# A two-layer hybrid decoder trunk: transposes and sums of gate logarithms moved from TensorE to VectorE, and the order of some projections and of w_out changed

## The chip, the cores and the metric

The kernel runs on one core of one Trainium2 chip. The metric is the device time of one execution in microseconds (us). Before the change it is 941.57 us, the median of three runs (941.54 to 941.61).

## The reference, cut to what matters

`x` has 256 rows of 2048. Each of two layers normalises the rows, multiplies them by `w_in` (2048 x 7700), sends the columns to four groups of four heads, gates each group's output, and multiplies the four outputs, side by side, by `w_out` (2048 x 2048):

```
h = rms_norm(x, norm_g);  p = split_columns(h @ w_in)
fox  = forgetting_attention(q, k, v, log_sigmoid(p["fox_f"] + fox_fb))       * silu(p["fox_g"])
diff = rms_norm((softmax(q1 k1^T) - lam * softmax(q2 k2^T)) v, diff_norm_g)  * silu(p["diff_g"])
moba = softmax(q k^T) v, causal (256 rows are one block of keys)             * silu(p["moba_g"])
gla  = rms_norm(gla_chunked(q, k, v, log_a), gla_norm_g)                     * silu(p["gla_g"])
       log_a = log_sigmoid(p["gla_a"] @ gla_wa2 + gla_ba) / 16
       inside a chunk: scores[t,s] = sum_d q[t,d] k[s,d] exp(cum[t,d] - cum[s,d]), cum = cumsum(log_a)
x = x + concat([fox, diff, moba, gla]) @ w_out
```

A last `rms_norm` with `final_norm_g` ends it. All of it is float32.

## The kernel before, in words

**Weights in steps.** The weights (160 MB) are read once, in 304 steps of at most 528 KB. A step holds two or four slabs of 128 rows of one block of columns (256 to 512 wide). Its raw slab is split in two rounded halves, `hi` (ScalarE, `hi_of`, line 399) and `lo` = raw - `hi` (VectorE, `lo_of`, line 402); the left side is split too (`hTp` for the normalised rows, `mTh` and `mTl` for the mixed groups). TensorE multiplies hi by hi, hi by lo and lo by hi into the PSUM tile `mm`. `raw`, `hi` and `lo` have four buffers each, and `prepare(i + 3)` is written ahead of `multiply` of step i, so the halves of a step are asked for three steps before TensorE reads them. A "rows" step of 512 columns is 12 matmuls of 512 columns; a "cols" step is 8 of 512 and 8 of 256.

**The order of the work.** Each engine works through its own list in the order in which the program was written, and that order is made in Python: the loop over `plan` (line 1369) writes prepare, settle (evacuates a finished block), multiply, and then `tick`, which lets each pending task (a generator) write a little more. `tick` lets tasks go on as long as the estimated work of VectorE and of ScalarE (`Costed`, line 176) is below a budget that grows with the estimated time of TensorE (`give_time`). A task that lacks an input stands at `until`. Steps of a layer come in the order of `_blocks`: gla, fox, diff, moba, then `w_out`; steps 0 to 151 are the first layer's, 152 to 303 the second's. A `w_out` block takes the groups in the order 3 (gla), 0 (fox), 1 (diff), 2 (moba).

**The side work.** What is not a weight matmul goes through two PSUM tiles called `side` (two banks each):

- `gla`, line 599: forms logarithms `gl` of the gates (rows by features), splits them in `gh` and `glo`, and multiplies both by the 0/1 matrix `a_r` (1152 columns, the constant "sets"), which gives for seven levels of halving the sum of logarithms between a row and its block's middle. ScalarE takes the exponential straight from PSUM into `ee`. VectorE multiplies it into q and k (`tq`, `ee`) and picks the scores with `masks`.
- Probabilities are transposed in `transposed_p` (line 753): on VectorE by `turned` (line 290, sixteen 32x32-block transposes for each group of tiles) when `by_rows` is true (fox alone), else as 12 transposes of 128x128 on TensorE (line 288) through `side`, which ScalarE and VectorE copy out.
- `finish_rows` (line 524) normalises and gates gla and diff; gla's result goes through `turned`, diff's through 8 TensorE transposes.
- `make_hT` (line 432) turns chunks of the residual rows `xs` for the next layer: chunks 0 to 2 on VectorE, chunk 3 on TensorE.

**The end.** The last block ("apart") finishes rows 0 to 127 first, then rows 128 to 255; `final_rows` (line 1135) adds the residual, sums squares, raises to -1/2 on GpSimd, scales 2048 columns on ScalarE and VectorE and sends them out in four pieces.

Of the kernel before, what the change touches and what calls it, by code (L numbers as in the profile page):

```python
# [13 lines left out]
F32 = mybir.dt.float32  # L14
F32R = mybir.dt.float32r
# [6 lines left out]
P = 128  # L22
SEQ = 256
D = 2048
# [38 lines left out]
def _constants():  # L63

    i = np.arange(P)
    tables, at = {"f": [], "b": []}, {}

    def put(name, a, kind="f"):
        parts = tables[kind]
        at[name] = (sum(x.shape[1] for x in parts), a.shape[1])  # L70
        parts.append(np.ascontiguousarray(a, TYPES[kind]))

    put("ident", np.eye(P))
    put("after", (i[:, None] > i[None, :]))
# [3 lines left out]
    sets, masks = [], []  # L78
    for h in GLA_LEVELS:
        blk, second = i // (2 * h), (i // h) % 2 == 1  # L80
        ref = blk * 2 * h + h - 1
        u, t = i[:, None], i[None, :]
        a = np.where(second[None, :], (u > ref[None, :]) & (u <= t), (u > t) & (u <= ref[None, :]))
        sets.append(a / GLA_TAU)
        masks.append(((blk[:, None] == blk[None, :]) & ~second[:, None])[:, second])
    sets += [(i[:, None] > i[None, :]) / GLA_TAU, (i[:, None] <= i[None, :]) / GLA_TAU]
    put("sets", np.concatenate(sets, 1), "b")
# [16 lines left out]
def _blocks():  # L104
# [6 lines left out]
    for l in range(DEPTH):  # L111
        for kind, c0, n in (
# [29 lines left out]
def _steps():  # L142

    steps = []
    for i, b in enumerate(_blocks()):
        per = b["per"]
        for j in range(0, KT, per):
            key = (j // 4, i) if i < 3 else (9, i)
            steps.append((key, len(steps), {"block": i, "kts": b["kts"][j:j + per], "first": j == 0, "last": j + per == KT,
                                           "odd": j // per % 2 == 1}))  # L150
    steps = [s for _, _, s in sorted(steps, key=lambda z: z[:2])]
    at = 0
    for s in steps:
        s["at"] = at
        at += P * len(s["kts"]) * _BLOCKS[s["block"]]["n"]
    return steps
# [61 lines left out]
def hybrid_trunk(  # L218
# [100 lines left out]
    ones_r = cp.tile([P, P], F32R, name="ones_r")  # L319
    a_r = cp.tile([P, (NL + 2) * P], F32R, name="a_r")  # L320
    neg_b = cp.tile([P, P], BF16, name="neg_b")
# [23 lines left out]
    def constants():  # L345
# [5 lines left out]
        s = []  # L351
        for name in ("sets", "upto", "masks"):
# [12 lines left out]
        yield  # L365
        v_.tensor_copy(a_r, s[0])
        v_.tensor_copy(upto_r, s[1])
        v_.tensor_copy(masks.rearrange("p l t -> p (l t)"), s[2])
        v_.tensor_scalar(ones_r, ident, 0.0, 1.0, op0=OP.mult, op1=OP.add)
# [154 lines left out]
    def finish_rows(l, gi, o, ops, scale, sg):  # L524
# [20 lines left out]
        yield  # L545
        if scale is None:
            t = yield from s4.take([P, H, SEQ])
            yield from turned(t.rearrange("p h (m t) -> p m h t", m=2), mixed.rearrange("p m (h d) -> p m h d", h=H))
            s4.put(mixed)
            yield from split_group(l, gi, t, lambda: s4.put(t))  # L550
            return
# [47 lines left out]
    def gla(l, an):  # L599
# [8 lines left out]
        al = yield from take_side()  # L608
        for m in range(2):
            matmul(al[:, m * 256:(m + 1) * 256], at17[:, m * P:(m + 1) * P], wa[:, l], True, True)  # L610
        yield
        e = yield from s2.take([P, 512])
        gl = yield from s2.take([P, 2, 256])
        yield from log_sigmoid(gl.rearrange("p m e -> p (m e)"), al[:, :512], e)
# [5 lines left out]
        yield  # L620
        glo = yield from s2.take([P, 2, 256], F32R)
        lo_of(glo, gl, gh)
        s2.put(gl)
# [20 lines left out]
        for pair in range(2):  # L644
            ee = yield from s8.take([P, 2, NL + 1, P])
            for m in range(2):
                pe = yield from take_side()
                for b in range(2):
                    for part in (gh, glo):
                        lhs = part[:, m, pair * P:(pair + 1) * P]  # L650
                        if b == 0:
                            matmul(pe[:, :512], lhs, a_r[:, 0:512], part is gh, part is glo)
                        elif m == 0:
                            matmul(pe[:, 512:], lhs, a_r[:, 512:1024], part is gh, part is glo)
                        else:
                            matmul(pe[:, 512:896], lhs, a_r[:, 512:896], part is gh, False)
                            matmul(pe[:, 896:], lhs, a_r[:, (NL + 1) * P:], False, part is glo)
                yield
                a_.activation(ee[:, m].rearrange("p l t -> p (l t)"), pe, AF.Exp)
                side.put(pe)  # L660
            yield
# [40 lines left out]
        s4.put(qkT)  # L702
        s2.put(gh, glo)
        yield from until(("gla_v", l))
# [87 lines left out]
    def attend_columns(l, gi, name, qT, kT, forget=None):  # L792
# [204 lines left out]
    def diff(l):  # L997
# [124 lines left out]
    def final_part(chunk, c):  # L1122
# [9 lines left out]
        for m in range(2):  # L1132
            v_.tensor_mul(xs[:, m, c], xs[:, m, c], fng[chunk][:, :c.stop - c.start])

    def final_rows(m, ps):
# [11 lines left out]
        a_.activation(xs[:, m, 1024:1536], xs[:, m, 1024:1536], AF.Copy, scale=r)  # L1147
# [4 lines left out]
        nc.scalar.dma_start(rows[:, 1024:1536], xs[:, m, 1024:1536])  # L1152
        v_.scalar_tensor_tensor(xs[:, m, c], xs[:, m, c], r, fng[3][:, 256:], op0=OP.mult, op1=OP.mult)
        v_.tensor_scalar(xs[:, m, 1536:D - 256], xs[:, m, 1536:D - 256], r, None, op0=OP.mult)
        nc.sync.dma_start(rows[:, 1536:], xs[:, m, 1536:])

    dones = []
    for l in range(DEPTH):
# [4 lines left out]
            started(diff, rotated("diff_k", "rope_d", DIFF_HALF, True)),  # L1163
            diff_gate,
            preceded(partial(turning, "rope_m"), rows_v("diff_v")),
            rotated("moba_q", "rope_m", MOBA_HALF, False),
            started(moba, rotated("moba_k", "rope_m", MOBA_HALF, True)),
            gate_columns("moba_g"), rows_v("moba_v"),
            residual(0), residual(1), residual(2), residual(3),
# [246 lines left out]
```

## Time and profile before

| | |
|---|---|
| median of three runs | 941.57 us |
| the profiled execution | 941.5 us, span of its trace 939.7 us |
| TensorE matmul (PE) | 929.9 us busy, 99% of the span, 5398 matmuls |
| TensorE weight load (PEld, beside the matmuls) | 816.1 us, 87% |
| VectorE (DVE) | 669.9 us, 71% |
| ScalarE (ACT) | 479.5 us, 51% |
| GpSimd (POOL) | 68.3 us, 7% |
| DMA | 170 MB, 181 GB/s over the span |

A busy share is a mean over 940 us: how much of an engine is free at one place is read in a stretch. Names such as `mm<-hi,hTp` give the tile written and the tiles read; line 188 is a helper through which every VectorE and ScalarE operation is recorded, so operations are told apart by tile and shape there.

### The profile page before, as it was taken

What the parts mean: (1) busy time and instruction counts of PE and PEld (TensorE: products, weight loads), DVE (VectorE), ACT (ScalarE), POOL (GpSimd) and SP (SyncE); (2) the same over time, 40 slices, a digit from 0 to 9 for tenths busy, and PEclk for the clock granted to TensorE, in tenths of its full rate; (3) what the DMA queues carried; (4) which work ended last, traced back from release to release, by engine and by line L of the source; (5) the groups of instructions that cost most, each with busy time, mean ns of one, the idle gap of its engine ahead of it and who ended that gap; (6) DMA issues with size and microseconds to landing.
All of it is one profiled execution on the core that took longest, in us unless ns stands there. A gap on an engine that the chain in (4) does not pass through costs nothing.

```text
span 939.7 us, 13910 instructions
## 1 busy us (share of the span) xinstructions
PE 929.9 (99%) x5398; PEld 816.1 (87%) x5398; DVE 669.9 (71%) x978; ACT 479.5 (51%) x651; POOL 68.3 (7%) x45
## 2 busy tenths in 40 slices
PE   9999999999999999999999999999999999999996
PEld 7989899889889888888899899898888888888886
DVE  7666787799856886588856667877985759755563
ACT  7675534453574446445556544456446544554451
POOL 0010201001110210000001102100111002100000
PEclk9999999999999999999999999999999999999999
DMA  8766555556555465566665545454555655755552
GB/s 307 230 198 210 187 180 166 162 178 187 178 186 179 135 212 174 163 188 186 202 182 173 166 141 168 151 198 154 162 180 191 202 157 177 231 175 173 188 177 90
DMA packets 49077, 170.20 MB, mean 181 GB/s; under 512 B 5969, under 2 KB 6513, under 8 KB 49010
## 3 DMA queue, kind: packets, MB, share of 16 engines
q1 hardware_dynamic: 46592, 165.24, 55.6%
q0 software_dynamic: 640, 2.10, 0.9%
q10 hardware_dynamic: 1778, 1.97, 0.7%
q8 instruction: 42, 0.69, 0.3%
q14 instruction: 25, 0.20, 0.1%
HBM read 167.19 MB, written 2.10 MB: 180 GB/s over the span
## 4 chain that ended last, share of the span: by engine, by line
PE 95%; DVE 2%; issue 1%; DMA 1%; ACT 0%; SPq 0%; POOLq 0%; POOL 0%; DVEq 0%; ACTq 0%
PE mm L284 86%; PE side L284 8%; PE side L288 1%; DVE lo L188 1%; DMA raw<-in_weights 1%; DVE four L188 0%; DVE hTp L188 0%; ACT hTp L188 0%; DVE xs L188 0%; ACT four L188 0%; ACT hi L188 0%; SPq L1193 0%; POOLq L1412 0%; POOL rf L397 0%; ACT two L188 0%
## 5 line engine op out<-in xcount | busy, mean ns | idle before, releaser
L188 DVE TENSOR_TENSOR lo<-raw,hi 128x1024 fp32r<-128x1024 f32 (+3 forms) x301 | 377.4, 1261 | 227.7 <-ACT hi L188 226.0
L188 ACT ACTIVATE hi<-raw 128x1024 fp32r<-128x1024 f32 (+3 forms) x301 | 318.0, 1059 | 401.8 <-PE mm L284 363.0
L284 PE MATMUL mm<-hTp,hi 128*128 128x512 f32 x1120 | 272.6, 393 | 0.0
L284 PEld LDWEIGHTS mm<-hTp,hi 128*128 128x128 f32 x1120 | 204.5, 188 | 39.4 <-issue 0.3
L284 PE MATMUL mm<-hi,hTp 128*128 128x512 f32 (+2 forms) x1024 | 196.6, 339 | 0.1
L284 PEld LDWEIGHTS mm<-hi,hTp 128*128 128x128 f32 x1024 | 159.8, 188 | 21.8 <-ACT hi L188 0.6
L284 PEld LDWEIGHTS mm<-hTp,lo 128*128 128x128 f32 x1120 | 144.7, 191 | 5.9
L284 PE MATMUL mm<-hTp,lo 128*128 128x256 f32 x1120 | 149.3, 284 | 0.0
L284 PE MATMUL mm<-lo,hTp 128*128 128x512 f32 (+2 forms) x512 | 104.9, 337 | 0.1
L284 PEld LDWEIGHTS mm<-lo,hTp 128*128 128x128 f32 x512 | 81.3, 188 | 10.4 <-DVE lo L188 0.3
L284 PE MATMUL mm<-hi,mTh 128*128 128x512 f32 (+1 forms) x256 | 64.8, 378 | 0.0
L284 PE MATMUL mm<-hi,mTl 128*128 128x512 f32 (+1 forms) x256 | 64.4, 376 | 0.0
L284 PE MATMUL mm<-lo,mTh 128*128 128x512 f32 (+1 forms) x256 | 64.4, 376 | 0.0
L284 PEld LDWEIGHTS mm<-hi,mTl 128*128 128x128 f32 x256 | 46.2, 188 | 8.8
L284 PEld LDWEIGHTS mm<-lo,mTh 128*128 128x128 f32 x256 | 46.2, 188 | 8.7
L284 PEld LDWEIGHTS mm<-hi,mTh 128*128 128x128 f32 x256 | 46.0, 188 | 8.5
L284 PE MATMUL side<-four,four 128*128 128x128 f32 (+1 forms) x320 | 38.3, 277 | 0.0
L284 PEld LDWEIGHTS side<-four,four 128*128 128x128 f32 (+1 forms) x320 | 35.0, 190 | 2.4 <-issue 1.4
L954 POOL TENSOR_TENSOR four<-four,two 128x1024 f32<-128x1024 f32 x8 | 20.8, 2594 | 218.1 <-DVE four L188 218.1
L188 ACT ACT_TABLE_LOAD x27 | 34.6, 1283 | 2.0 <-DVE an L188 1.5
L188 DVE STREAM_TRANSPOSE four<-four 32x256 f32<-32x256 f32 x64 | 27.9, 436 | 1.0
L188 DVE TENSOR_TENSOR both<-mm,both 128x512 f32<-128x512 f32 x35 | 23.9, 683 | 0.0
(162 smaller groups left out, 638.6 us busy)
## 6 DMA issues: line engine op xcount, KB each, us to landing
raw<-in_weights SPq DMA_DIRECT2D x272, 512.0 KB, 3.9
raw<-in_weights SPq DMA_DIRECT2D x16, 516.0 KB, 3.9
raw<-in_weights SPq DMA_DIRECT2D x15, 528.0 KB, 4.2
xs<-in_x SPq DMA_DIRECT2D x4, 512.0 KB, 4.6
four<-in_xt SPq DMA_DIRECT2D x3, 512.0 KB, 6.7
out<-xs SPq DMA_DIRECT2D x6, 256.0 KB, 3.0
two<-in_const POOLq DMA_DIRECT2D x4, 256.0 KB, 3.4
two<-in_final_norm_g POOLq DMA_DIRECT2D x4, 256.0 KB, 5.7
```

The costliest lines, as they stand in the source:

```text
L188: return f(*args, **kw)
L284: t_.matmul(out, lhsT, rhs, start=start, stop=stop)
L288: t_.transpose(out, src, ident)
L954: g_.tensor_mul(sw, sw, over(f[:, 1], H))
```

## The change

Five edits:

1. **gla.** `a_r`, `gh` and `glo` go. The gate projection is made with features on partitions, `tensor_tensor_scan` on VectorE forms the running sums `F` (four scans of 128 columns in a layer), and for each pair of heads 15 subtractions of 128 columns on VectorE give the differences for the seven levels (60 in all). ScalarE takes their exponentials from SBUF, in three operations for a pair.
2. **Transposes.** `transposed_p` is called with `by_rows` true for moba and diff too, and diff's `finish_rows` uses `turned`.
3. **make_hT.** Chunk 2 goes to TensorE (8 transposes, second layer only).
4. **Order.** `diff_v` is projected after `moba_k` (with its gate's table task moved along), and the first two `w_out` blocks run together: groups 3, 0, 1 of the first, the same of the second, then group 2 (moba) of the first and of the second.
5. **The end.** The sum of squares of the earlier columns is prepared (`base`), the last columns are multiplied by the gain ahead of the power, and rows leave in three pieces: 768 columns from ScalarE, twice 640 from VectorE.

```diff
@@ _blocks
             ("rows", COL["diff_g"], 512),
-            ("rows", COL["diff_v"], 512),
             ("cols", COL["moba_q"], 512),
             ("cols", COL["moba_k"], 512),
+            ("rows", COL["diff_v"], 512),
@@ _steps
             key = (j // 4, i) if i < 3 else (9, i)
+            if b["w"] == "w_out" and b["c0"] < 1024:
+                key = (9, i - b["c0"] // 512, j >= 12, i)
@@ make_hT
-        if chunk < 3:
+        if chunk < 2:
             t = yield from s4.take([P, 4, SEQ])
@@ finish_rows
-        if scale is None:
-            t = yield from s4.take([P, H, SEQ])
...
-        ps = yield from transposes(mixed)
+        t = yield from s4.take([P, H, SEQ])
+        yield from turned(t.rearrange("p h (m t) -> p m h t", m=2), mixed.rearrange("p m (h d) -> p m h d", h=H))
         s4.put(mixed)
-        yield
-        yield from split_group(l, gi, ps.rearrange("p (h t) -> p h t", h=H), lambda: side.put(ps))
+        yield from split_group(l, gi, t, lambda: s4.put(t))
@@ gla
-        gh = yield from s2.take([P, 2, 256], F32R)
-        hi_of(gh, gl)
...
+        F = yield from s2.take([P, 2, 2, P])
+        for pair in range(2):
+            for m in range(2):
+                v_.tensor_tensor_scan(F[:, pair, m], one.to_broadcast([P, P]), gl[:, pair, m * P:(m + 1) * P], 0.0,
+                                      op0=OP.mult, op1=OP.add)
...
-                            matmul(pe[:, :512], lhs, a_r[:, 0:512], part is gh, part is glo)
...
-                a_.activation(ee[:, m].rearrange("p l t -> p (l t)"), pe, AF.Exp)
...
+            for i, h in enumerate(GLA_LEVELS):
+                f = F[:, pair].rearrange("p m (b two h) -> p m b two h", two=2, h=h)
+                z = ee[:, :, i].rearrange("p m (b two h) -> p m b two h", two=2, h=h)
+                mid = f[:, :, :, 0, h - 1:h].to_broadcast([P, 2, 64 // h, h])
+                v_.tensor_sub(z[:, :, :, 0], mid, f[:, :, :, 0])
+                v_.tensor_sub(z[:, :, :, 1], f[:, :, :, 1], mid)
...
+            a_.activation(ee[:, 0], ee[:, 0], AF.Exp, scale=1.0 / GLA_TAU)
+            a_.activation(ee[:, 1, :NL], ee[:, 1, :NL], AF.Exp, scale=1.0 / GLA_TAU)
+            a_.activation(ee[:, 1, NL], F[:, pair, 1], AF.Exp, scale=1.0 / GLA_TAU)
@@ attend_columns
-        pt, release = yield from normalised(p0, p1, su, name == "fox")
+        pt, release = yield from normalised(p0, p1, su, True)
@@ diff
-        pt, release = yield from transposed_p(p0[:, 0], p1[0], False, s4, p0)
+        pt, release = yield from transposed_p(p0[:, 0], p1[0], True, s4, p0)
@@ final_rows
-        ss = sm.tile([P, 1], F32, name="ssf", bufs=2)
-        v_.tensor_reduce(ss, parts[:, m], axis=AX.X, op=OP.add)
-        t = before_pow(ss, 1, 1.0 / D)
+        v_.tensor_scalar(t, parts[:, m, 4:5], 1.0 / D, env["base"][:, m:m + 1], op0=OP.mult, op1=OP.add)
+        v_.tensor_mul(xs[:, m, c], xs[:, m, c], fng[3][:, 256:])
...
+        a_.activation(xs[:, m, 1280:], xs[:, m, 1280:], AF.Copy, scale=r)
+        nc.scalar.dma_start(rows[:, 1280:], xs[:, m, 1280:])
         for i in range(2):
-            q = slice(i * 512, (i + 1) * 512)
+            q = slice(i * 640, (i + 1) * 640)
...
-        v_.scalar_tensor_tensor(xs[:, m, c], xs[:, m, c], r, fng[3][:, 256:], op0=OP.mult, op1=OP.mult)
-        v_.tensor_scalar(xs[:, m, 1536:D - 256], xs[:, m, 1536:D - 256], r, None, op0=OP.mult)
-        nc.sync.dma_start(rows[:, 1536:], xs[:, m, 1536:])
```

How the instructions move, at three places. First TensorE in the first layer's gla, where the first pair's sums of logarithms stood between weight matmuls (`two` holds `gh` and `glo`). Before:

```order
L284 MATMUL side_818<-a_r,two_747 128x512
L284 MATMUL side_818<-a_r,two_767 128x512
L284 MATMUL side_818<-a_r,two_747 128x512
L284 MATMUL side_818<-a_r,two_767 128x512
L284 MATMUL mm<-hi,hTp 128x512 x8
L284 MATMUL mm<-lo,hTp 128x512 x4
L284 MATMUL side_842<-a_r,two_747 128x512
L284 MATMUL side_842<-a_r,two_767 128x512
L284 MATMUL side_842<-a_r,two_747 128x384
L284 MATMUL side_842<-a_r,two_747 128x128
L284 MATMUL side_842<-a_r,two_767 128x384
L284 MATMUL side_842<-a_r,two_767 128x128
```

Now:

```order
L281 MATMUL side_768<-ct,two_748 128x2 x4
L281 MATMUL mm<-hi,hTp 128x512 x8
L281 MATMUL mm<-lo,hTp 128x512 x4
L281 MATMUL mm<-hi,hTp 128x512 x8
L281 MATMUL mm<-lo,hTp 128x512 x4
```

Ten matmuls for each pair and layer are gone; the weight steps follow each other.

Second VectorE in the first layer's diff, from the reciprocals of the softmax sums on (`four_2532` and `four_2682`, later `four_2537` and `four_2722`, hold the probabilities). Before:

```order
L188 RECIPROCAL rs<-su 128x8 x2
L188 TENSOR_TENSOR nr<-rs,su 128x8
L188 TENSOR_SCALAR nr<-nr,lam 128x8
L188 SCALAR_TENSOR_TENSOR four_2532<-four_2532,nr 128x128 x4
L188 TENSOR_TENSOR lo<-raw,hi 128x1024
L188 SCALAR_TENSOR_TENSOR four_2682<-four_2705,nr,four_2682 128x256 x4
L188 TENSOR_TENSOR lo<-raw,hi 128x1024
L188 TENSOR_TENSOR two_2765<-two_2765,rb 128x512
L188 TENSOR_TENSOR lo<-raw,hi 128x1024 x2
L188 TENSOR_TENSOR both<-mm,both 128x512
L188 STREAM_SHUFFLE four_2861<-both 128x512
L188 TENSOR_TENSOR four_2860<-both,two_2765 128x512
```

Now:

```order
L185 SCALAR_TENSOR_TENSOR four_2722<-four_2749,nr,four_2722 128x256 x4
L185 TENSOR_TENSOR lo<-raw,hi 128x1024
L185 STREAM_TRANSPOSE two_2864<-four_2537 32x4x32 x4
L185 TENSOR_TENSOR lo<-raw,hi 128x1024
L185 STREAM_TRANSPOSE two_2864<-four_2537 32x4x32 x4
L185 TENSOR_TENSOR four_2666<-four_2666,four_2667 128x1024
L185 TENSOR_TENSOR lo<-raw,hi 128x1024
L185 TENSOR_TENSOR both<-mm,both 128x512
L185 STREAM_SHUFFLE four_2903<-both 128x512
L185 TENSOR_TENSOR four_2902<-both,two_2573 128x512
L185 STREAM_TRANSPOSE two_2864<-four_2537 32x4x32 x4
L185 TENSOR_TENSOR lo<-raw,hi 128x1024
```

Groups of four transposes now stand between the `lo` of one step and that of the next; eight such groups, 32 transposes, run from step 90 to step 99.

Third TensorE in the first layer's `w_out`, from the product of moba's probabilities and values (`side0`) on; mm_3592 is the first block's tile before, mm_3610 and mm_3744 are the first's and the second's now. Before:

```order
L284 MATMUL side0_3643<-two1_3605,four7_3589 128x128
L284 MATMUL mm_3592<-hi_3583,mTh_114 128x512 x4
L284 MATMUL mm_3592<-hi_3583,mTl_115 128x512 x4
L284 MATMUL mm_3592<-lo_3584,mTh_114 128x512 x4
L284 MATMUL mm_3592<-hi_3607,mTh_114 128x512 x4
L284 MATMUL mm_3592<-hi_3607,mTl_115 128x512 x4
L284 MATMUL mm_3592<-lo_3608,mTh_114 128x512 x4
L284 MATMUL mm_3592<-hi_3625,mTh_114 128x512 x4
L284 MATMUL mm_3592<-hi_3625,mTl_115 128x512 x4
L284 MATMUL mm_3592<-lo_3626,mTh_114 128x512 x4
L284 MATMUL mm_3592<-hi_3656,mTh_114 128x512 x4
L284 MATMUL mm_3592<-hi_3656,mTl_115 128x512 x4
```

Now:

```order
L281 MATMUL side0_3797<-four5_3689,four6_3607 128x128 x2
L281 MATMUL mm_3744<-hi_3738,mTh_113 128x512 x4
L281 MATMUL mm_3744<-hi_3738,mTl_114 128x512 x4
L281 MATMUL mm_3744<-lo_3739,mTh_113 128x512 x4
L281 MATMUL mm_3744<-hi_3761,mTh_113 128x512 x4
L281 MATMUL mm_3744<-hi_3761,mTl_114 128x512 x4
L281 MATMUL mm_3744<-lo_3762,mTh_113 128x512 x4
L281 MATMUL mm_3744<-hi_3779,mTh_113 128x512 x4
L281 MATMUL mm_3744<-hi_3779,mTl_114 128x512 x4
L281 MATMUL mm_3744<-lo_3780,mTh_113 128x512 x4
L281 MATMUL mm_3610<-hi_3810,mTh_113 128x512 x4
L281 MATMUL mm_3610<-hi_3810,mTl_114 128x512 x4
```

In both, three steps stand between that product and the first step that reads moba's group (hi_3656, hi_3810). The product itself stood behind the third step of `w_out` and stands behind the ninth now.

## Rows read from the trace of the kernel before

**Rows 1.** The page: busy time by engine, granted TensorE clock, chain by engine

```profile
PE 929.9 (99%) x5398; PEld 816.1 (87%) x5398; DVE 669.9 (71%) x978; ACT 479.5 (51%) x651; POOL 68.3 (7%) x45
...
PEclk9999999999999999999999999999999999999999
...
PE 95%; DVE 2%; issue 1%; DMA 1%; ACT 0%; SPq 0%; POOLq 0%; POOL 0%; DVEq 0%; ACTq 0%
```

**Rows 2.** Waits of PE, all of them: who waited for whom, us, times, longest

```profile
PE side L338 <- DVE four L333: 1.3, 1, 1.3
PE side L284 <- DVE four L188: 0.7, 1, 0.7
```

**Rows 3.** Chain in order of time: start us, us, what

```profile
73.40 0.93 PE side L284 x4
...
77.06 0.99 PE side L284 x6
...
98.29 2.79 PE mm L284 x16
...
290.09 0.87 PE side L288 x8
...
293.77 0.44 PE side L288 x4
...
471.94 0.88 PE side L288 x8
```

**Rows 4.** Timeline, PE just behind side matmuls, and one step later

```profile
252.04 2.11 PE L284 MATMUL mm<-hi,hTp 128*128 128x512 f32 x8
...
254.90 1.98 PE L284 MATMUL mm<-hi,hTp 128*128 128x512 f32 x8
...
257.62 1.98 PE L284 MATMUL mm<-hi,hTp 128*128 128x512 f32 x8
```

**Rows 5.** Groups of VectorE by shape: count, busy us, mean ns, idle before

```profile
L188 DVE TENSOR_TENSOR lo<-raw,hi 128x1024 fp32r<-128x1024 f32 x268 | 337.5, 1267 | 199.9 <-ACT hi L188 198.4 <-issue 0.3
L188 DVE STREAM_TRANSPOSE four<-four 32x256 f32<-32x256 f32 x64 | 27.9, 436 | 1.0
L188 DVE TENSOR_TENSOR both<-mm,both 128x512 f32<-128x512 f32 x35 | 23.9, 683 | 0.0
...
L188 DVE STREAM_TRANSPOSE two<-two 32x128 f32<-32x128 f32 x32 | 9.7, 302 | 0.5
...
L188 DVE TENSOR_TENSOR eight<-eight,four 128x128 f32<-128x128 f32 x36 | 7.9, 284 | 0.0
...
L188 DVE COPY two<-side 128x512 f32<-128x512 f32 x4 | 2.7, 684 | 0.0
L188 DVE TENSOR_TENSOR two<-two,two 128x512 fp32r<-128x512 f32 x2 | 2.5, 1236 | 0.0
```

**Rows 6.** Windows of 20 and 40 us: busy time of each engine in each

```profile
110.00:130.00 20.00, 20.00 (x126) 17.98 (x125) 19.52 (x44) 7.58 (x8) 2.17 (x2) 1.00 0.66 211
640.00:680.00 40.00, 40.00 (x235) 35.49 (x234) 37.77 (x62) 20.19 (x24) 2.69 (x1) 1.00 0.55 171
```

**Rows 7.** Timeline where `w_out` comes to moba's group, first layer

```profile
393.09 1.23 DVE L188 TENSOR_TENSOR lo<-raw,hi 128x1024 fp32r<-128x1024 f32 x1 [1.70 <-ACT hi L188]
...
397.00 1.22 DVE L188 TENSOR_TENSOR mTl<-four,mTh 128x1024 fp32r<-128x1024 f32 x1
...
398.14 1.07 PE L284 MATMUL mm<-hi,mTh 128*128 128x512 f32 x4
...
399.05 1.07 PE L284 MATMUL mm<-hi,mTl 128*128 128x512 f32 x4
...
400.86 1.07 PE L284 MATMUL mm<-hi,mTh 128*128 128x512 f32 x4
```

**Rows 8.** Timeline of the end, rows 128 to 255

```profile
933.02 0.16 DVE L188 TENSOR_REDUCE ssf<-parts 128x1 f32<-128x5 f32 x1 [0.57 <-ACT two L188]
933.22 0.15 DVE L188 TENSOR_SCALAR pw<-ssf 128x1 f32<-128x1 f32 x1
...
934.04 0.88 DVE L188 TENSOR_SCALAR xs<-xs,rf 128x512 f32<-128x512 f32 x2 [0.67 <-POOL rf L397]
...
935.61 0.33 SPq L1155 DMA_DIRECT2D out<-xs  x1
```

More of the change, by code (lines that the diff above doesn't have):

```diff
@@ L77, in _constants @@
     put("neg", np.where(i[None, :] > i[:, None], NEG, 0.0), "b")
-    sets, masks = [], []
+    masks = []
     for h in GLA_LEVELS:
         blk, second = i // (2 * h), (i // h) % 2 == 1
[L81 to L84, printed above, removed]
         masks.append(((blk[:, None] == blk[None, :]) & ~second[:, None])[:, second])
-    sets += [(i[:, None] > i[None, :]) / GLA_TAU, (i[:, None] <= i[None, :]) / GLA_TAU]
-    put("sets", np.concatenate(sets, 1), "b")
     put("masks", np.concatenate(masks, 1), "b")
@@ L319, in hybrid_trunk @@
     ones_r = cp.tile([P, P], F32R, name="ones_r")
-    a_r = cp.tile([P, (NL + 2) * P], F32R, name="a_r")
     neg_b = cp.tile([P, P], BF16, name="neg_b")
@@ L351, in constants @@
         s = []
-        for name in ("sets", "upto", "masks"):
+        for name in ("upto", "masks"):
             c, n = CAT[name]
@@ L365, in constants @@
         yield
-        v_.tensor_copy(a_r, s[0])
-        v_.tensor_copy(upto_r, s[1])
-        v_.tensor_copy(masks.rearrange("p l t -> p (l t)"), s[2])
+        v_.tensor_copy(upto_r, s[0])
+        v_.tensor_copy(masks.rearrange("p l t -> p (l t)"), s[1])
         v_.tensor_scalar(ones_r, ident, 0.0, 1.0, op0=OP.mult, op1=OP.add)
@@ L545, in finish_rows @@
         yield
-        if scale is None:
-            t = yield from s4.take([P, H, SEQ])
[L548 to L551, printed above, removed]
-        ps = yield from transposes(mixed)
+        t = yield from s4.take([P, H, SEQ])
+        yield from turned(t.rearrange("p h (m t) -> p m h t", m=2), mixed.rearrange("p m (h d) -> p m h d", h=H))
         s4.put(mixed)
-        yield
-        yield from split_group(l, gi, ps.rearrange("p (h t) -> p h t", h=H), lambda: side.put(ps))
+        yield from split_group(l, gi, t, lambda: s4.put(t))
     def log_sigmoid(dst, xin, e):
@@ L608, in gla @@
         al = yield from take_side()
-        for m in range(2):
-            matmul(al[:, m * 256:(m + 1) * 256], at17[:, m * P:(m + 1) * P], wa[:, l], True, True)
+        for pair in range(2):
+            matmul(al[:, pair * SEQ:(pair + 1) * SEQ], wa[:, l, pair * P:(pair + 1) * P], at17, True, True)
         yield
         e = yield from s2.take([P, 512])
-        gl = yield from s2.take([P, 2, 256])
-        yield from log_sigmoid(gl.rearrange("p m e -> p (m e)"), al[:, :512], e)
+        gl = yield from s2.take([P, 2, SEQ])
+        yield from log_sigmoid(gl.rearrange("p a t -> p (a t)"), al[:, :512], e)
         s2.put(e)
@@ L617, in gla @@
         yield
-        gh = yield from s2.take([P, 2, 256], F32R)
-        hi_of(gh, gl)
-        yield
-        glo = yield from s2.take([P, 2, 256], F32R)
-        lo_of(glo, gl, gh)
+        F = yield from s2.take([P, 2, 2, P])
+        for pair in range(2):
+            for m in range(2):
+                v_.tensor_tensor_scan(F[:, pair, m], one.to_broadcast([P, P]), gl[:, pair, m * P:(m + 1) * P], 0.0,
+                                      op0=OP.mult, op1=OP.add)
         s2.put(gl)
@@ L645, in gla @@
             ee = yield from s8.take([P, 2, NL + 1, P])
[L646 to L651, printed above, removed]
-                            matmul(pe[:, :512], lhs, a_r[:, 0:512], part is gh, part is glo)
[L653 to L658, printed above, removed]
-                a_.activation(ee[:, m].rearrange("p l t -> p (l t)"), pe, AF.Exp)
-                side.put(pe)
+            for i, h in enumerate(GLA_LEVELS):
[4 more added lines that the diff above has]
+                v_.tensor_sub(z[:, :, :, 1], f[:, :, :, 1], mid)
+                if i % 3 == 2:
+                    yield
+            v_.tensor_sub(ee[:, 0, NL], F[:, pair, 0, P - 1:].to_broadcast([P, P]), F[:, pair, 0])
+            yield
+            a_.activation(ee[:, 0], ee[:, 0], AF.Exp, scale=1.0 / GLA_TAU)
+            a_.activation(ee[:, 1, :NL], ee[:, 1, :NL], AF.Exp, scale=1.0 / GLA_TAU)
+            a_.activation(ee[:, 1, NL], F[:, pair, 1], AF.Exp, scale=1.0 / GLA_TAU)
             yield
@@ L702, in gla @@
         s4.put(qkT)
-        s2.put(gh, glo)
+        s2.put(F)
         yield from until(("gla_v", l))
@@ L1133, in final_part @@
             v_.tensor_mul(xs[:, m, c], xs[:, m, c], fng[chunk][:, :c.stop - c.start])
+        if chunk == 3:
+            yield
+            base = sm.tile([P, 2], F32, name="base", bufs=1)
+            v_.tensor_reduce(base, parts[:, :, 0:4], axis=AX.X, op=OP.add)
+            v_.tensor_scalar(base, base, 1.0 / D, EPS, op0=OP.mult, op1=OP.add)
+            env["base"] = base
     def final_rows(m, ps):
@@ L1140, in final_rows @@
         square_sum(parts, m, c, 4)
-        ss = sm.tile([P, 1], F32, name="ssf", bufs=2)
-        v_.tensor_reduce(ss, parts[:, m], axis=AX.X, op=OP.add)
-        t = before_pow(ss, 1, 1.0 / D)
+        t = sm.tile([P, 1], F32, name="tf", bufs=2)
+        v_.tensor_scalar(t, parts[:, m, 4:5], 1.0 / D, env["base"][:, m:m + 1], op0=OP.mult, op1=OP.add)
+        v_.tensor_mul(xs[:, m, c], xs[:, m, c], fng[3][:, 256:])
         r = sm.tile([P, 1], F32, name="rf", bufs=2)
@@ L1163, in hybrid_trunk @@
             started(diff, rotated("diff_k", "rope_d", DIFF_HALF, True)),
-            diff_gate,
-            preceded(partial(turning, "rope_m"), rows_v("diff_v")),
+            preceded(partial(turning, "rope_m"), diff_gate),
             rotated("moba_q", "rope_m", MOBA_HALF, False),
             started(moba, rotated("moba_k", "rope_m", MOBA_HALF, True)),
+            rows_v("diff_v"),
             gate_columns("moba_g"), rows_v("moba_v"),
```

2 lines of the change are left out of this document (removed).

## The prediction

> **What bounds the kernel now.** I read the page first. TensorE is busy 99% of the span at the full granted clock (ten tenths, 2.4 GHz), and 95% of the chain that ended last is its own work [rows 1]. A busy matmul record could hide waiting, so I read two more views. The list of all waits of TensorE's matmuls has two entries, 2.0 us together [rows 2]; both lie in the first 30 us. In the timeline, steady steps of 512 columns follow each other at 2.72 us for 12 matmuls (254.90 to 257.62), 227 ns for one [rows 4]; the step of 16 matmuls takes 2.79 us in the chain [rows 3]. So from about 30 us to 926 us TensorE never stands still, and a microsecond of work taken off it is a microsecond of the kernel, as long as the halves `hi` and `lo` and the mixed groups still come in time. They come from VectorE, and 71% over the span [rows 1] says little about that: in some stretches VectorE is at 98% (19.52 of 20 us) or 94% (37.77 of 40) and TensorE is still 100% busy [rows 6]. The lead explains it. The `lo` that starts at 393.09 and ends at 394.32 belongs to the step that begins at 400.86 [rows 7]: 6.5 us in hand. VectorE may fall behind by about that much, in one stretch, at no cost.
>
> **The change part by part.** The sum stands against the profiled execution, 941.5 us (span 939.7 and 1.8 around it); the median is 941.57, so 0.07 is added at the end.
>
> *Sums of logarithms.* For each pair of heads and layer the chain holds one piece of 4 matmuls, 0.93 us, and one of 6, 0.99 us [rows 3]: 1.92. Four such pairs: **-7.7 us**. Nothing replaces them on TensorE; the gate projection keeps its two matmuls, turned round.
>
> *Transposes on TensorE.* Eight take 0.87 us, four 0.44 [rows 3]. In a layer moba's probabilities are 8 + 4, diff's 8 + 4, diff's result 8: 3 x 0.87 + 2 x 0.44 = 3.49, twice 6.98. Chunk 2 adds eight in the second layer, 0.88 as those of chunk 3 [rows 3]. **-6.1 us**.
>
> *Returning from side work.* The first eight matmuls behind a side group take 2.11 us, later ones 1.98 [rows 4]: 0.13 us, lost when TensorE changes over. A layer loses nine groups (five of transposes, four of sums), chunk 2 adds one: 17 groups, **-2.2 us**. A returning group may also cost as little as nothing where its neighbours stay; I take 0.10 each, -1.7, and keep 0 to -2.2 for the range.
>
> *VectorE's new work.* 32 transposes of 32x128 in a layer at 302 ns and 48 of 32x256 at 436 ns, less 16 of the latter for chunk 2: 64 x 0.302 + 80 x 0.436 = 54.2 us. The 60 subtractions are like the 128x128 product, 284 ns: 17.0 us. The eight scans have no row; they lie between 284 ns (one pass over 128 columns) and 1.24 us (the dearest row here that VectorE writes rounded, 512 columns): 2.3 to 9.9 us; I take 0.4 each, 3.2, as the rows rise little from 128 columns to 256. Copies out of PSUM (4 x 0.684) and the two `lo` of the gates (2 x 1.236) go: -5.2 [rows 5]. Together +69 us, so VectorE has 739 of about 926 us, 80%. As a mean that is covered; what matters is one stretch.
>
> *The densest stretch.* Steps 88 to 99 (diff's differences and transposes, moba's q and k, diff_v) ask VectorE for: 12 `lo` at 1.267 = 15.2; three evacuations of three operations at about 0.70 = 6.3; eight multiply-adds of 128 and 256 columns, estimated at 0.35 from the rows of 128 and 512, 2.8; small operations 0.9; one addition of 1024 columns 1.27; 16 transposes at 0.302 = 4.8 and 16 at 0.436 = 7.0. Sum 38.3 us. TensorE needs 8 x 2.79 + 4 x 2.72 = 33.2. VectorE falls 5.1 us behind, within 6.5. Then come four steps with little but `lo` (5.1 of 10.9 us), and it is back. The second layer repeats it. Gla's stretch (steps 28 to 39) gains 34 operations of 0.28 to 0.4 us in a layer over some 20 steps, and TensorE loses 3.85 there; by the same tally VectorE asks for 2 us more than TensorE, also within the lead. So waits are costed at nothing in principle; as 5.1 is not far from 6.5, I put **+0.5 us** for short ones.
>
> The Trainium skill speaks against this move: "VectorE: DVE Perf Modes", in Rules for kernel authors, sends a 128x128 transpose to TensorE where its result may lie in PSUM. In engine time the rows agree: eight cost 0.87 us there and 16 x 0.436 = 7.0 us on VectorE. By that rule the change would lose; by the chain it gains, because the engine that it relieves is the one that never waits.
>
> *ScalarE.* It loses four copies of 1024 columns and the gates' `hi`, and works off the exponentials of a pair in one burst of three; at 51% [rows 1] I cost it at nothing. Its cover is the same lead: `hi` is written three steps ahead too.
>
> *The order.* diff_v moves behind moba_k: the same steps, weights and DMAs in another sequence; diff's product of probabilities and values, which needs it, also comes later, and diff's group is finished six steps before `w_out` reads it. In `w_out`, moba's group is read from the 13th step instead of the 7th. The product behind it moved by six steps as well, so the margin stays what it was: `mTl` ends at 398.22 and is first read at 399.05, 0.8 us [rows 7]. SP's queue carries the same weight loads in the new order; behind them queues nothing but the next. No gain and no loss.
>
> *The end.* The reduction goes (933.02 to 933.22 [rows 8]: 0.20). Behind the power, VectorE has two operations of 640 columns instead of 2 x 512 and two of 256, and the last DMA is issued about 0.4 us earlier than 935.61. But a megabyte still has to leave, starting when the first piece is ready, and that piece is larger, 640 columns for 512 (0.44 us, half of 0.88 [rows 8], becomes about 0.55). Bounds: 0.1 lost, 0.6 gained; I take **-0.3**, in between.
>
> Sum: -7.7 - 6.1 - 1.7 + 0.5 - 0.3 = -15.3; 941.5 + 0.07 - 15.3 = **926.3 us**. With the bounds of the small terms alone: 924.9 (0.3 more at the end, 0.5 more at returns, no waits, 0.1 of rounding) to 928.4 (nothing at the returns, 0.1 lost at the end).
>
> **The rivals.**
>
> 1. *VectorE late in the dense stretches.* If the lead is one step smaller than read (2.7 us; ScalarE, whose exponentials wait for VectorE's maxima, can hold up `hi` behind them), 5.1 us against 3.8 lets TensorE wait 1.3 us in each layer, and gla's and moba's stretches add as much or twice that at the worst: 3 to 7 us given back, 929 to 933. For it: 98% stretches exist already. Against it: those cost nothing [rows 2, 6], and the surplus of 5.1 is built up over twelve steps, in which the lead is read off a step that was not even pressed [rows 7]. Chance 0.20.
>
> 2. *Moba's group late at `w_out`.* With VectorE behind by over 0.8 us at that place, the 13th step of `w_out` waits for `mTl`, at most a step, 2.7 us, in each layer: 929 to 932. For it: a thin margin [rows 7], and 32 transposes of moba shortly before. Against it: between the last transposes and the use lie some five steps of little VectorE work. Chance 0.06.
>
> 3. *VectorE sets the pace: slower than before.* One mechanism: in each group of four steps in which VectorE is asked for more than TensorE, TensorE pays the surplus. Place: steps 28 to 39, 84 to 99 and 108 to 115 of a layer, `w_out`'s chunks. Price: adding the surpluses over all groups by the durations above, an estimated 22 us without any lead, so 926 + 22 = 948. It decides against the change from the point where the lead hides less than about 7 of these 22. For it: the rule above. Against it: by the same tally, an estimate as well, the kernel before has some 15 us of surplus and pays none [rows 2]. Chance 0.03.
>
> 4. *TensorE is not the bound, so the change doesn't bring what it takes off.* Weight loads are busy 87% [rows 1], and if the gap to 100% were slack, the removed work would turn into waiting: 941.5. The Trainium skill ("Perfetto Trace Analysis", Identifying the Most-Contended Engine) would rather read that share than the matmuls' 99%. Against it: steps at an even 2.72 us and no waits [rows 2, 4]. Chance 0.02.
>
> **How the numbers follow.** The forecast (waits under 2 us) has 0.69. The likeliest time is 926.3. The range 924.6 to 930.8 takes in the bounds of the small terms and the lower half of rivals 1 and 2, and leaves out at most 2 in 10. 0.2% is 1.9 us, about what a measurement here tells from no change. Forecast, rivals 1 and 2 are all faster by more: 0.95; rival 4 is no change: 0.02; rival 3 slower: 0.03.
>
> **What would show it.** In the profile of the changed kernel TensorE should again be 98 to 99% busy, with 96 matmuls fewer (4 x 10 sums and 64 transposes out, 8 in), no waits of PE beyond 30 us longer than 0.3 us, VectorE at about 739 us and 288 stream transposes. A PE wait on `lo` or on ACT `hi` at steps 88 to 104 (about 250 to 290 us and 700 to 740 us) speaks for rival 1, one on `mTl` for rival 2, waits of over 20 us in sum for rival 3. A 512-column step that takes longer than 2.72 us away from those waits would prove the reading of TensorE wrong, and a subtraction or scan of over 0.6 us my VectorE prices.

## The result, and the profile after

The changed kernel takes 931.60 us (median of 4 runs, 931.27 to 933.12) against 941.59 of the kernel before, measured beside it: a ratio of 0.9893, interval 0.9878 to 0.9907. It is faster, by 10.0 us and not by the 15.3 that were forecast; the range ended 0.8 us below the result. The profiled execution took 931.93 us, span 930.2.

The page of the changed kernel, as [rows 1]:

```profile
PE 918.1 (99%) x5302; PEld 803.1 (86%) x5302; DVE 739.7 (80%) x1181; ACT 469.7 (50%) x646; POOL 70.4 (8%) x45
...
PE 94%; DVE 2%; DMA 1%; issue 1%; ACT 0%; SPq 0%; POOLq 0%; POOL 0%; DVEq 0%; ACTq 0%
```

TensorE is still the bound, has 96 matmuls fewer and 11.8 us less to do; VectorE has the 739 us that were forecast. What is new stands in the waits of TensorE (engine, line, what it waited for: us in total, times, longest); [rows 2] had two entries:

```profile
PEld mm L281 <- DVE lo L185: 2.5, 6, 0.5
...
PE side L281 <- DVE eight L185: 1.8, 2, 1.6
...
PE mm L281 <- ACT hi L185: 0.3, 1, 0.3
```

Beside these stand the two entries on `four` of [rows 2], as they were. The waits on `lo` appear with TensorE's weight loads (PEld), since `lo` is the weight there, and not with its matmuls. The longest new wait is on `eight`, the operands of the gated linear attention's products. The wait on `hi` stands at 5.2 us, ahead of everything that the change touches, and is missing in the lists of several runs below; I leave it out. The chain in order of time (start us, us, what) shows how it comes about, in the first layer:

```profile
113.64 0.96 ACT hi L185
...
121.14 1.23 DVE lo L185
...
123.61 0.30 DVE eight L185
...
123.95 1.16 PE side L281 x8
```

From 114.6 to 123.9 the chain is VectorE's work, one piece behind the other, and the last operand is ready when TensorE has long finished the step ahead of the product. Where VectorE falls behind stands in the timeline ahead of it (start us, us, engine, operation, tile):

```profile
103.65 2.79 POOL L885 TENSOR_TENSOR four<-ct,fh 128x512 fp32r<-128x512 f32 x2 [30.92 <-ACT fh L185]
...
104.41 2.99 DVE L185 TENSOR_TENSOR eight<-two 128x128 f32<-128x128 f32 x6
...
107.55 3.41 POOL L885 TENSOR_TENSOR four<-ct,fl 128x512 fp32r<-128x512 f32 x2 [1.11 <-DVE fl L185]
...
109.98 1.53 DVE L185 TENSOR_TENSOR eight<-two 128x128 f32<-128x128 f32 x3
...
111.54 1.90 ACT L185 ACTIVATE eight<-eight 128x1024 f32<-128x1024 f32 x2 [1.64 <-DVE eight L185]
...
114.63 1.22 DVE L185 TENSOR_TENSOR lo<-raw,hi 128x1024 fp32r<-128x1024 f32 x1 [1.31 <-ACT hi L185]
```

Of the 60 subtractions 56 take about 0.28 us, and four take 1.12 to 2.49, each beside a GpSimd operation. Three of the four lie here (104.41, 105.46, 109.98) and cost VectorE 2.5 us. ScalarE waits 1.64 us for the last subtraction, its burst of exponentials then stands ahead of the next two `hi`, and VectorE stands 1.31 us for the first of these before it goes on. The windows (stretch, its us, busy PE, PEld, DVE, ACT, POOL, then granted clock, DMA share, GB/s) show what is lost at this place, 1.6 of 20 us. At the next one, in the second line, TensorE counts as busy for 19.88 of 20 us, and the loss shows only in the length of its steps:

```profile
110.00:130.00 20.00, 18.44 (x115) 16.26 (x114) 18.23 (x44) 8.72 (x10) 0.96 (x1) 1.00 0.66 215
310.00:330.00 20.00, 19.88 (x94) 15.91 (x93) 18.23 (x24) 7.84 (x9) 2.68 (x1) 1.00 0.61 207
```

The second place is at the end of diff's transposes, 320 us and, the same again, 777 us. (The expectations below call them moba's; moba's run from 374 to 396 us.) The timeline there (start us, us, engine, operation, tile; GpSimd, then VectorE, then TensorE):

```profile
311.18 2.68 POOL L943 TENSOR_TENSOR four<-four,two 128x1024 f32<-128x1024 f32 x1 [24.03 <-DVE four L185]
```

```profile
311.52 3.42 DVE L185 TENSOR_TENSOR lo<-raw,hi 128x1024 fp32r<-128x1024 f32 x1
314.98 1.78 DVE L185 STREAM_TRANSPOSE four<-four 32x256 f32<-32x256 f32 x4
...
319.86 1.23 DVE L185 TENSOR_TENSOR lo<-raw,hi 128x1024 fp32r<-128x1024 f32 x1
```

```profile
316.24 1.97 PE L281 MATMUL mm<-hi,hTp 128*128 128x512 f32 x8
318.07 1.20 PE L281 MATMUL mm<-lo,hTp 128*128 128x512 f32 x4
319.10 1.98 PE L281 MATMUL mm<-hi,hTp 128*128 128x512 f32 x8
321.14 1.19 PE L281 MATMUL mm<-lo,hTp 128*128 128x512 f32 x4
322.18 2.00 PE L281 MATMUL mm<-hi,hTp 128*128 128x512 f32 x8
```

The `lo` that ends at 321.09 is used at 321.14: no lead is left. From start to start the three steps take 2.86, 3.08 and 3.08 us (316.24, 319.10, 322.18, 325.26) for 2.72 each: 0.86 us, and 0.87 in the second layer. Ahead of it, the `lo` that stands beside GpSimd's multiplication takes 3.42 us for 1.23. So the waits are 1.8 at `eight` and 1.7 at `lo`: 3.5 us, where the sum had 0.5.

These three steps are the last of diff_v's eight, steps 96 to 103, which run from 302.64 to 325.26 us: between moba_k and moba's gate only diff_v multiplies with the weights on the left (`mm<-hi,hTp`). So the waits stand right behind the stretch that my tally named, steps 88 to 99; the 250 to 290 us that the prediction gave for it are over 30 us too early.

VectorE's new groups, as [rows 5] (the shape, count | busy us, mean ns; the four long subtractions and one scan of 1.49 us, also beside GpSimd, lift the means, and the other seven scans take about 0.40):

```profile
L185 DVE STREAM_TRANSPOSE four<-four 32x256 f32<-32x256 f32 x160 | 69.7, 435 | 2.5
...
L185 DVE TENSOR_TENSOR eight<-two 128x128 f32<-128x128 f32 x60 | 17.8, 361 | 0.0
...
L185 DVE TENSOR_TENSOR_SCAN two<-one,two 128x128 f32<-128x128 f32 x8 | 3.8, 538 | 0.0
```

The end, as [rows 8]:

```profile
923.34 0.21 DVE L185 TENSOR_SCALAR tf<-parts,base 128x1 f32<-128x1 f32 x1 [0.58 <-ACT two L185]
...
923.64 0.67 POOL L392 TENSOR_TENSOR rf<-tf,halfpow 128x1 f32<-128x1 f32 x1 [5.01 <-DVE tf L185]
...
924.34 1.02 DVE L185 TENSOR_SCALAR xs<-xs,rf 128x640 f32<-128x640 f32 x2 [0.45 <-POOL rf L392]
```

### The profile page after: what moved, and what is told of

Its sections match the earlier page's. It is cut to its first block, busy times and chain, and to the rows that moved or that the text cites. A ratio compares the mean times of both kernels' runs of the same rounds, so it can differ in the third digit from the quotient of the medians.

```text
span 930.2 us, 13911 instructions
## 1 busy us (share of the span) xinstructions
PE 918.1 (99%) x5302; PEld 803.1 (86%) x5302; DVE 739.7 (80%) x1181; ACT 469.7 (50%) x646; POOL 70.4 (8%) x45
## 4 chain that ended last, share of the span: by engine, by line
PE 94%; DVE 2%; DMA 1%; issue 1%; ACT 0%; SPq 0%; POOLq 0%; POOL 0%; DVEq 0%; ACTq 0%
PE mm L281 86%; PE side L281 8%; DVE lo L185 1%; DMA four<-in_xt 1%; DMA raw<-in_weights 1%; DVE four L185 0%; DVE tq L185 0%; PE side L285 0%; ACT hi L185 0%; DVE hTp L185 0%; DVE xs L185 0%; SPq L1185 0%; POOLq L1404 0%; POOL rf L392 0%; DVE both L185 0%
## 5 line engine op out<-in xcount | busy, mean ns | idle before, releaser
L281 PE MATMUL mm<-hTp,lo 128*128 128x256 f32 x1120 | 147.3, 283 | 0.0
L185 DVE STREAM_TRANSPOSE four<-four 32x256 f32<-32x256 f32 x160 | 69.7, 435 | 2.5
```

What stands on the lines that cost most here:

```text
L185: return f(*args, **kw)
L281: t_.matmul(out, lhsT, rhs, start=start, stop=stop)
```

## The experiments

All start from the changed kernel, and each was timed beside the kernel before (medians 941.49 to 941.77). Theories: the miss is made of the waits at `eight` (VectorE's backlog meets operands made one step ahead), the waits at `lo` (GpSimd has held VectorE up), and terms of the sum that TensorE does not have (the returns, the end). Rival: the four parts cost or bring something else than the sum says.

### Undoing one part at a time

**The sums of log f back on TensorE** (`a_r`, `gh`, `glo` and their ten matmuls for a pair, as in the kernel before).

> The changed kernel (931.6 us) with the sums of log f back on TensorE and everything else of the change kept. My sum: 7.7 us of matmuls come back, and if the two waits at gla's products (1.72 us at 122.0, 0.36 us at 531.0) are there only because VectorE works off the new subtractions, they go: 931.6 + 7.7 - 2.1 = 937.2. If returning from side work costs what I put on it, 8 groups x 0.10 more: 938.0. Rival, the waits stay because VectorE is late for another reason: 939.3 or more.

Measured: 938.0 us (ratio 0.9960, 0.9947 to 0.9972). The part is worth 6.4 us. The list of waits of TensorE's matmuls has nothing on `eight` any more:

```profile
PE side L341 <- DVE four L336: 1.3, 1, 1.3
PE side L287 <- DVE four L191: 1.1, 1, 1.1
```

So the wait at `eight` comes with the subtractions. What share of it GpSimd has, which stretches three of them, was not tried. Whether a return costs 0.10, this run can't tell: 937.2 and 938.0 are within its spread (937.22 to 939.52).

**The transposes back on TensorE** (`by_rows` false for moba and diff, `transposes` in diff's `finish_rows`, chunk 2 on VectorE).

> The changed kernel with all its moved transposes (moba's and diff's probabilities, diff's result, chunk 2 the other way) back where they were. By the times from one start to the next in the two traces 64 transposes were worth 6.2 us and the 8 added 0.8; the waits on lo at moba's transposes (about 0.65 us a layer) go: 931.6 + 5.4 - 1.3 = 935.7. By the terms of my sum, 6.1 and nine returns at 0.10: 931.6 + 6.1 + 0.9 - 1.3 = 937.3. If the waits on lo have another cause than these transposes: 1.3 more than either.

Measured: 950.78 us (1.0095, 1.0081 to 1.0109), 13 us or more above either figure. The expectation was wrong. TensorE's waits show why:

```profile
PE side L285 <- DVE four L185: 3.9, 4, 1.2
PE mm L281 <- ACT gate L185: 3.8, 1, 3.8
PE side L281 <- DVE eight L185: 3.2, 3, 1.6
```

TensorE's own transposes now wait for their sources, four times, and the second layer begins 3.8 us late. The latter belongs to chunk 2 (below), which this run turns the other way: of the 19.2 us above the changed kernel, chunk 2 alone is worth 8.5, so the run gives no price of the other transposes.

**Both edits of the order undone** (`diff_v` ahead of `moba_q`, `w_out`'s first blocks one after the other).

> The changed kernel with diff_v and w_out's first two blocks in the old order. My sum put the order at nothing: 931.6, and the same waits. Rival: the order is what keeps moba's and diff's groups in time now that VectorE makes them, so without it TensorE waits for mTl or the probabilities at w_out, up to a step of 2.7 us in each layer: 933 to 937.

Measured: 961.17 us (1.0201, 1.0186 to 1.0215). The rival is right, and by far more than it said: without the new order the change would make the kernel 19.4 us slower. The waits, the place on VectorE and TensorE, and the windows of that stretch:

```profile
PE side L279 <- DVE four L183: 16.8, 3, 8.0
PE mm L279 <- ACT mTh L183: 4.8, 2, 2.4
```

```profile
391.37 7.17 DVE L183 STREAM_TRANSPOSE four<-four 32x256 f32<-32x256 f32 x16
```

```profile
398.60 1.22 PE L279 MATMUL side<-four,four 128*128 128x128 f32 x4 [8.03 <-DVE four L183]
```

```profile
390.00:400.00 10.00, 1.89 (x9) 1.70 (x9) 8.13 (x18) 0.20 (x1) 0.00 (x0) 0.73 0.32 102
400.00:410.00 10.00, 7.60 (x27) 6.50 (x26) 2.45 (x2) 1.13 (x2) 0.00 (x0) 0.50 0.00 0
410.00:420.00 10.00, 10.00 (x42) 8.20 (x41) 4.88 (x5) 4.13 (x4) 0.00 (x0) 0.92 0.40 110
```

The planner issues four transposes in a step, so moba's 32 need eight steps, 21.8 us. In the old order `w_out` reaches moba's group before that; the last 16 are then issued in one go, TensorE waits 8.0 us for them and 2.4 for the group behind them, and comes out of it at half the clock.

**`w_out`'s order alone undone** (the `key` of the first two blocks).

> The changed kernel (931.6 us) with w_out's first two blocks in the old order, diff_v where the change puts it. With both order edits undone it was 961.2, with waits of 8.1 us at moba's product and 2.7 us on mTh in each layer. Theory: those waits belong to w_out's order alone, since moba's 32 transposes then lie between the last projection and the block's seventh step: 958 to 961. Rival: diff_v's place carries them, as diff's transposes push moba's back: 932 to 936.

Measured: 953.06 us (1.0122, 1.0103 to 1.0141), below the expected 958: the larger part, 21.5 us, is `w_out`'s, but not all.

```profile
PE side L279 <- DVE four L183: 9.0, 3, 4.2
PE mm L279 <- ACT mTh L183: 4.8, 2, 2.4
```

**`diff_v`'s place alone undone.**

> The changed kernel with diff_v in its old place alone. My sum put it at nothing: 931.6. If w_out's order carries the whole of the 29.5 us that both edits are worth, also 931.6. Rival: diff_v behind moba_k is what lets VectorE work off diff's transposes, and TensorE waits at diff's or moba's products without it: 933 to 937.

Measured: 938.44 us (0.9963, 0.9951 to 0.9976): 6.8 us, by the wait for moba's group, not by diff's products as the rival had it:

```profile
PE mm L281 <- ACT mTh L185: 4.8, 2, 2.4
```

With `diff_v` behind them, moba's q and k come four steps earlier, and so do its softmax and transposes. The two edits are worth 21.5 and 6.8 us one by one, 29.5 together: they give the same chain its time.

**Chunk 2 back on VectorE** (`if chunk < 3` in `make_hT`).

> The changed kernel with chunk 2 of the second layer's input turned on VectorE again, as before. By my sum TensorE loses 8 transposes: 930.7. By the trace of the run with all transposes put back, where TensorE waited 4.0 us at 496.6 for ScalarE's gate and 0.4 us at the row statistics: 931.6 - 0.8 + 4.7 = 935.5; then the eight transposes on TensorE were there to have the second layer begin in time.

Measured: 940.11 us (0.9980, 0.9971 to 0.9989): 8.5 us, more than the 3.9 that I had read off the other run. On VectorE the turning takes four steps, so the row statistics of the second layer come late. In the chain TensorE stands from 490.27 to 494.08 behind the first group's evacuation, which queues behind a `hi` and a `lo`:

```profile
490.29 1.06 ACT hi L185
...
491.38 1.23 DVE lo L185
...
492.78 0.48 ACT gate L185
...
494.08 2.08 PE mm L281 x4
```

Behind it come a stretch at a granted clock of 0.58 (495 to 500 us) and longer waits at `eight` in the second layer (3.2 us in all instead of 1.8).

**The old end.**

> The changed kernel with the old end. My sum gave the new end 0.3 us: 931.9. The trace after shows the time from TensorE's end to the last instruction 0.1 us longer than before: 931.5. Either way within 0.3 us of 931.6; over 932.2 would mean that the end is worth more than both.

Measured: 931.81 us (0.9894, 0.9880 to 0.9907). That is 0.2 us more than the changed kernel, well within the runs' spread (931.30 to 933.50 against 931.27 to 933.12): no gain is shown.

### Taking the waits away

**A step more before the products.**

```diff
             v_.tensor_mul(ee[:, 1, NL], ee[:, 1, NL], qv[:, 1])
+            yield
             for m in range(2):
```

> The changed kernel (931.6 us) with one step more between VectorE's last products of the gated linear attention and TensorE's use of them. Theory: the waits of 1.72 us (at 122.0) and 0.36 us (at 531.0) are there because these operands are made one step ahead and VectorE is a step behind there; with a step more they go: 929.5. Rival: VectorE's backlog is only handed on to the next lo or group: 931.6.

Measured: 930.37 us (0.9886, 0.9872 to 0.9901). No wait on `eight` is left; in the second layer there is a new one of 1.0 us on `four` at 576.03, so the gain is 1.2 us instead of 2.1. The times alone don't show it, as the runs overlap (929.76 to 932.21 against 931.27 to 933.12); the list of waits does.

**moba_k's product with the sines on VectorE.**

```diff
-                g_.tensor_mul(sw, sw, over(f[:, 1], H))
+                (v_ if name == 'moba_k' else g_).tensor_mul(sw, sw, over(f[:, 1], H))
```

> The changed kernel with one operation of each layer moved from GpSimd to VectorE: the product of moba_k's swapped columns with the sines, 128x1024. It runs at 311.5 and 768.0, and the lo beside it takes 3.43 us instead of 1.23, so VectorE loses 2.2 us by it and would need about 1.27 for the product itself. Theory: the waits on lo at moba's transposes (320.7, 323.8, 777.2, 780.2; 0.65 us a layer) come from those 2.2 us: 931.6 - 1.3 = 930.3 or a little above, as VectorE gains only 0.9. Rival: VectorE is late there by its 32 transposes alone: 931.6, the waits as they are.

Measured: 929.82 us (0.9876, 0.9860 to 0.9893). The same `lo`, at the same place:

```profile
311.25 1.23 DVE L185 TENSOR_TENSOR lo<-raw,hi 128x1024 fp32r<-128x1024 f32 x1
...
323.90 1.22 DVE L185 TENSOR_TENSOR four<-four,two 128x1024 f32<-128x1024 f32 x1
```

VectorE does 1.22 us more work there and is earlier all the same. The list of TensorE's waits has no entry on `lo` left, that on `eight` is as it was (1.7 us). The theory stands, with a gain of 1.8 us for the expected 1.3: the three longer steps of each layer had cost 1.7. The stretching alone isn't enough: the changed kernel has four more `lo` of 3.43 us (at 213.53, 237.24, 670.62 and 693.68), and TensorE waits for none of them. At most one group of four transposes follows close behind these, and three follow the ones at 311.52 and 767.98.

**Both.**

> Both of the last two edits. If both causes are right and independent: 931.6 - 2.1 - 1.3 = 928.2. If neither is: 931.6.

Measured: 928.64 us (0.9864, 0.9850 to 0.9879). The two gains add up (1.2 + 1.8 = 3.0 us): the causes are independent, and the new wait in the second layer stays.

### The price of a return

```diff
+        if s["first"] and b["kind"] == "cols" and s["block"] is not blocks[1] and s["block"] is not blocks[2]:
+            for k in range(8):
+                t_.transpose(ps[:, k * P:(k + 1) * P], ident, ident)
```

> The changed kernel with added work: 8 transposes of the identity on TensorE ahead of the first matmul of 34 blocks of columns, into the block's own result buffer, overwritten there. It measures what a group of 8 costs with the change to it and back. If a group costs its 8 x 0.109 and nothing more: 34 x 0.87 = 29.6, so 961.2, or down to 958.2 as the waits of 3 us are covered by the longer steps. If each return costs 0.10 more, as my sum took it: 3.4 more, 961.6 to 964.6. In the trace the price of one group is read directly, from the last matmul before it to the thirteenth after it.

Measured: 958.57 us (1.0191, 1.0174 to 1.0209). That is 27.0 us more than the changed kernel; with the waits that the added work covers (up to 3.5 us) 27.0 to 30.5, or 0.79 to 0.90 us a group. With the returns it would be 0.97. One such group in the timeline:

```profile
104.48 2.01 PE L281 MATMUL mm<-hTp,hi 128*128 128x512 f32 x8
106.33 1.03 PE L1297 MATMUL mm<-ct 128*128 128x128 f32 x8
107.12 2.07 PE L281 MATMUL mm<-hTp,hi 128*128 128x512 f32 x8
109.03 2.08 PE L281 MATMUL mm<-hTp,lo 128*128 128x256 f32 x16
```

From the group's start to the next weight matmul it is 0.79 us, not 0.87; the eight behind it then take 1.91 (107.12 to 109.03) instead of 1.82. Together 0.88: the 0.09 us of the return are in the 0.87 already.

### A version from the findings

```diff
+            if l == 0:
+                yield
```

with moba_k's product on VectorE as above.

> A version made from the findings: the changed kernel with moba_k's product of sines on VectorE, and the step more before the products of the gated linear attention in the first layer only, as in the second it made a wait of 1.18 us (at 573.8) in place of one of 0.36. The run with both in both layers gave 928.6; 0.8 less is 927.8. Rival: the wait at 573.8 has another cause than the step: 928.6.

Measured: 928.19 us (927.79 to 928.28; ratio 0.9854, 0.9839 to 0.9870). The interval lies below that of the change, so it beats both kernels. Of the new waits 0.2 us is left:

```profile
PE side L281 <- DVE eight L185: 0.2, 1, 0.2
```

## Why the prediction was wrong

**The bound: right.** TensorE is busy 99%, and what was taken off it came off the time as long as VectorE was in time.

**Sums of logarithms and transposes: right in size.** Putting the sums back costs 6.4 us, which is 7.7 less the 1.8 of waits that the subtractions had cost, within 0.5. A group of eight transposes is worth 0.79 to 0.90 us, as the 0.87 had it.

**"Returning from side work" (-1.7): wrong, and a double count.** The 0.13 us were read from records that overlap, 2.11 us against 1.98 [rows 4]. The duration of a group in the chain [rows 3] holds them. The lower end, nothing, was the truth: 1.7 us of the miss.

**"Waits are costed at nothing in principle" (+0.5): wrong, the step that failed.** I read the lead off one calm step, 6.5 us [rows 7], and gave it to all of VectorE's output. That lead belongs to `lo` alone. The operands of the gated linear attention have one step of 2.7 us, and the wait stands there. `lo` did use up its lead, in steps 101 to 103, right behind the stretch that my tally named and within the steps that the prediction gave as a sign of its first rival. The tally had VectorE 5.1 us behind there and left out a resource: while GpSimd multiplies, VectorE's operations stretch, `lo` from 1.23 to 3.42 us, and in the same stretch the 128x8 product `nr` (285.10) takes 2.07 us, for 0.17 in the kernel before. With these 4.1 the surplus would be 9.2, past the 6.5; the 0.86 us that TensorE waited in each layer is less than that, so the tally, an estimate, is too high elsewhere. In the gated linear attention's stretch four subtractions took 1.12 to 2.49 us for the 0.28 that I took. ScalarE, costed at nothing under the same lead, belongs to that chain too: its burst waits for the subtractions and makes `hi` late. Waits of 3.5 us instead of 0.5 are 3.0 us of the miss; the last version takes all but 0.2 of those at `eight` and all at `lo` away, and is 3.4 us faster.

**The end (-0.3): no gain shown.** 0.2 by the run, within its spread, and nothing by the trace: the reduction is gone, but the operation ahead of the power takes 0.21 us for 0.15 [rows 8] and the power 0.67, for 0.56 in the trace of before, and a megabyte still has to leave.

Together 1.7 + 3.0 + 0.1 to 0.3 = 4.8 to 5.0 of the 5.3 us; the rest lies within the runs' spread. As a check, the sum without returns and with the last version's waits is 941.57 - 7.7 - 6.1 + 0.2 - 0.2 = 927.8, and that version takes 928.19.

**"The order: no gain and no loss": right as a term, wrong as a statement.** The reason that I gave, that the margin at moba's group stays what it was, misses that 32 transposes at four a step take 21.8 us of the plan. The order is the cover of that: without it the kernel is 29.5 us slower. The same holds for chunk 2, which I booked as 0.88 us lost and which saves 8.5. Both should have been named as the work that hides a term, with its price.

**The rivals.** The first (VectorE late in dense stretches, 929 to 933, chance 0.20) is what happened, by its mechanism, within its range and at two of its places, gla's products and diff's steps; moba's cost nothing. The lead that is a step shorter, its condition, holds for gla's operands; for `lo` it was GpSimd that took nearly a step. The others did not come. Once the order is undone the kernel is slower (961.2), but not as the third had it, by a surplus in every group of steps: TensorE stands at moba's group ahead of `w_out`, the second rival's place, for 8.0 and 2.4 us in each layer where that rival had at most 2.7.

The Trainium skill, "VectorE: DVE Perf Modes", Rules for kernel authors, would leave a 128x128 transpose on TensorE. With the old order the changed kernel goes the way of that rule, 961.2 us against 941.8; with the new one the transposes on VectorE are part of a gain, and taking them back costs 19.2 us, 8.5 of them by chunk 2, which goes the other way.

## What to carry to other kernels

A lead is a property of each operand and place, not of an engine: before booking a wait at nothing, look up for each consumer how many steps ahead its operand is issued, and how many steps the producer's work is spread over; and count what GpSimd does in that stretch against VectorE. A part of a change that costs nothing in the sum may be what pays for the rest, so price it by what happens without it. Add up start to start, not busy records, when matmuls overlap.

## What the runs showed of the hardware

**VectorE and GpSimd hold each other up.** Beside a GpSimd multiplication of 2.68 us (311.18 to 313.86) `lo` starts at 311.52 and ends at 314.94, 1.08 us after GpSimd: it did nearly all of its 1.23 us of work after the other had finished. The Trainium skill, "SBUF — State Buffer", SBUF: two separate sides, describes this as an exclusive lock between GpSimd and a VectorE operation with two inputs in SBUF, held for a whole instruction; the trace agrees. With that multiplication taken off GpSimd the same `lo` takes 1.23 us. So a 128x1024 product that costs VectorE 1.22 us itself costs it 2.19 when GpSimd does it at the wrong moment. It goes the other way round too: GpSimd's 128x1024 product of `ct` and `dgs` takes 1.90 us in the kernel before and with the sums back on TensorE; in the changed kernel six subtractions run beside it at 69.84 and it takes 2.88, and twelve beside the one at 511.40, which takes 5.17.

**A wait of TensorE can cost more than its length.** Behind the 8.0 us wait the granted clock is 0.50 (1.2 GHz) for the ten us from 400 to 410, and 0.92 in the next ten. Behind the 2.4 us waits without `diff_v`'s move it was 1.00 in the first layer and 0.66 for five us in the second, in one and the same execution:

```profile
412.00:416.00 4.00, 3.94 (x17) 3.10 (x17) 1.46 (x2) 1.06 (x1) 0.00 (x0) 1.00 0.02 4
...
870.00:875.00 5.00, 5.00 (x16) 3.67 (x15) 1.43 (x2) 1.06 (x1) 0.00 (x0) 0.66 0.00 0
```

Behind the 1.6 us wait of the changed kernel the clock stays at 1.00. What decides between the two levels was not tried.
